# Two products of 512 columns in place of four of 256 in each step of a modulation projection

## The chip, the cores and the metric

The kernel runs on one core of a Trainium2 chip. The metric is the device time in microseconds (us) of one execution. Engines are named as in the profile: PE is the matrix engine (its array is used here as a whole or in four quarters of 32 columns each), PEld is its loading of weights, DVE, ACT and POOL are the vector, scalar and general engines, SP is the engine that issues the loads from memory in its own order.

## What is computed

Two transformer blocks of width 2048 on 256 tokens. The change touches one piece of the second block, the modulation vectors: two rows (the vectors `c` and `c_ctx` after silu) times one matrix of 2048 x 12288 numbers in float32, some 100 MB that are read once.

```python
mod = jax.nn.silu(c) @ mod_w + mod_b
mod_c = jax.nn.silu(c_ctx) @ mod_w + mod_b
sh1, sc1, g1, sh2, sc2, g2 = jnp.split(mod[:, None, :], 6, axis=-1)
csh1, csc1, cg1, csh2, csc2, cg2 = jnp.split(mod_c[None, None, :], 6, axis=-1)
```

## The kernel before

A scheduler orders the instructions of each engine when the program is built; on the chip each engine works through its own list and waits on semaphores.

Most of the work is projections (`proj_t`, `proj_k`, `proj_n`, with `mm3` at L166 to L173): weights come in pieces of 128x1024 (L140), ACT copies each half into a rounded high part (L230), DVE takes the rest as a low part (L231), and PE makes three products for each 128x128 block of weights.

The modulation is filler between these projections. It is a generator, `modulation`, with 12 groups (`q`) of 1024 output columns; a group is 16 steps (`k`), one for each 128 rows of the matrix, so there are 192 steps. A step loads one tile `mw` of 128x1024 (L889; there are two such buffers, so step k's load waits until step k - 2 has been multiplied) and multiplies it by `scw`, 128 rows of 32 columns of which two hold the data and the rest zeros. The weights are thus 32 columns wide, and each of the step's four products of 256 columns stands on its own quarter of the array (`tile_position=(0, 32 * j)`) and writes its own 32 partitions of one accumulator `mps`. A float32 product is two instructions in the trace, two passes over the same columns, so a step is 8 matmul instructions.

After 16 steps ACT copies `mps` to `mrow` (L894), two small products with the identity turn the rows into columns (L897), and DVE adds the bias (L902).

Ten groups are asked for in the first block, by `tick` (two or three steps after each projection), and the last two in the MLP's first half (`MR = 3` steps after each pair of blocks of `w1m`). The first ten run between about 39 and 1000 us, the last two between 2635 and 2776 us.

Of the kernel before, what the change touches and what calls it, by code (L numbers as in the profile page):

```python
# [9 lines left out]
F32 = mybir.dt.float32  # L10
# [7 lines left out]
MUL, ADD, SUB = ALU.mult, ALU.add, ALU.subtract  # L18
# [3 lines left out]
NK = 16  # L22
# [11 lines left out]
PP, S0, S1 = 3, 3, 2  # L34
# [16 lines left out]
def bc(ap, n, axis):  # L51

    l = [list(x) for x in ap.ap]
    l.insert(axis, [0, n])
    return bass.AP(tensor=ap.tensor, offset=ap.offset, ap=l)


class Env:
    def __init__(self, tc, ctx):
        self.tc, self.nc = tc, tc.nc  # L60
        p = lambda name, bufs, **k: ctx.enter_context(tc.tile_pool(name=name, bufs=bufs, **k))
        self.cp = p("consts", 1)
        self.wp = p("weights", 3)
        self.hp = p("acts", 1)
        self.kp = p("work", 2)
        self.dp = p("dram", 1, space=bass.MemoryType.DRAM)
        self.ps = p("psum", 1, space=PSUM)

        self.slot, self.npt, self.held = None, 0, 0
# [773 lines left out]
class Second:  # L843


    def __init__(self, e, a):
        self.e, self.a, nc = e, a, e.nc
        v, g = nc.vector, nc.gpsimd
        c = lambda n, shape, dt=F32: e.cp.tile(shape, dt, name=n, tag=n)
        pv = c("pv2", [128, NPV2])  # L850
        nc.sync.dma_start(pv, a["pv2"])
        self.pv = {n: pv[:, i:j] for n, (i, j) in PV2.items()}
        self.modx, self.modc = c("modx", [128, 96]), c("modc", [128, 32])

        self.scw = c("scw", [128, 16, 32])
        g.memset(self.scw, 0.0)
        for j, n in enumerate(("c", "cc")):
            t = c("silu_" + n, [128, 16])
            nc.scalar.activation(t, self.pv[n], AF.Tanh, scale=0.5)
            v.scalar_tensor_tensor(t, t, 1.0, self.pv[n], op0=ADD, op1=MUL)  # L860
            v.tensor_scalar(self.scw[:, :, j], t, 0.5, None, op0=MUL)

        self.om, self.mu4, self.mu2 = c("om", [128, 28]), c("mu4", [128, 28, 4]), c("mu2", [128, 28, 2])
        mu = self.pv["mu"]
        v.tensor_scalar(self.om, mu, -1.0, 1.0, op0=MUL, op1=ADD)
        v.tensor_tensor(self.mu4, bc(mu, 4, 2), bc(self.pv["m4"], 28, 1), op=MUL)
        v.tensor_tensor(self.mu2, bc(mu, 2, 2), bc(self.pv["m2"], 28, 1), op=MUL)
        d = lambda n, k: e.dp.tile([128, k, T], F32, name=n, tag=n)
        self.zc, self.zx = d("zc", 24), d("zx", 24)
        self.gc, self.gx = d("gcd", 24), d("gxd", 24)  # L870
        self.gz, self.gate, self.x1 = d("gzd", 8), d("gated", 32), d("x1d", 16)
        self.ya, self.yb = d("yad", 8), d("ybd", 8)
        self.at = e.dp.tile([128, 2, 16, 128], F32, name="atd", tag="atd")
        self.twe = {s: c("twe" + s, [97, T]) for s in "cx"}
        self.xa = {s: c("xa" + s, [128, T]) for s in "cx"}
        self.ab = {s: c("ab" + s, [128, 2, 32]) for s in "cx"}
        self.xg = c("xg", [128, 2, T])
        self.state = [d(f"rws{b}", 1) for b in range(4)]


    def modulation(self, mp, groups):


        e, nc = self.e, self.e.nc
        for q in groups:
            ps = e.ps.tile([128, 512], F32, name="mps", tag="s1", bufs=S1)[:, :256]
            for k in range(NK):
                w = mp.tile([128, 1024], F32, name="mw", tag="mw", bufs=2)
                nc.sync.dma_start(w, self.a["mod_w"][k * 128:k * 128 + 128, q * 1024:(q + 1) * 1024])  # L889
                for j in range(4):  # L890
                    nc.tensor.matmul(ps[32 * j:32 * j + 32], self.scw[:, k, :], w[:, j * 256:(j + 1) * 256], start=k == 0, stop=k == NK - 1, tile_position=(0, 32 * j))  # L891
                yield
            rows = mp.tile([128, 256], F32, name="mrow", tag="mrow", bufs=1)
            nc.scalar.copy(rows, ps)  # L894
            p = e.pt()
            for i in range(2):
                nc.tensor.matmul(p[:, 8 * i:8 * i + 8], rows[:, i * 128:(i + 1) * 128], e.ident.rearrange("p (j r) -> p r j", j=4)[:, :2], start=True, stop=True)  # L897
            sl = slice(8 * q, 8 * q + 8)
            by = lambda x: x.rearrange("p (j i) -> p i j", i=2)
            pv = p[:, :16].rearrange("p (i m j) -> p i m j", i=2, m=2)  # L900
            for m, out in enumerate([self.modx] + ([self.modc] if q < 4 else [])):
                nc.vector.tensor_tensor(by(out[:, sl]), pv[:, :, m], by(self.pv["mod_b"][:, sl]), op=ADD)  # L902

# [1034 lines left out]
```

## Time and profile before

| | |
|---|---|
| median of 3 runs | 3372.09 us (3361.31 to 3379.54) |
| the profiled execution's own time | 3366.81 us |
| its span, first to last instruction | 3365.1 us |
| mean granted clock of PE | 0.985 of full speed |
| busy share of PE, DVE, ACT, POOL | 97%, 70%, 47%, 10% |
| moved to and from memory | 640.73 MB, 190 GB/s over the span |

A row of the profile names line, engine, operation, the tile written and those read. Durations are of one instruction; matmuls of one engine overlap in time, so what one costs is read from the start of one piece to the start of the next. In the timeline, neighbouring equal instructions are merged and counted (x8).

### The profile page before, as it was taken

To read this page: it belongs to the slowest core of one execution; us is meant where nothing else is said; L and a number is where in the kernel's file an instruction comes from. 1 tells how busy PE (TensorE), PEld (TensorE's weight loads), DVE (VectorE), ACT (ScalarE), POOL (GpSimd) and SP (SyncE) were. 2 spreads that over 40 slices of the span, in tenths; PEclk is the share of its full clock that TensorE was granted. 3 is DMA by queue.
4 is the path that set the end of the run, shared out by engine and by line. 5 is a ranking of instruction groups with operands and counts; after the bars stand their busy time and mean duration, and the time that the engine had idled before them with its cause. 6 is when DMAs were issued, how large, how long until landed. Compare 5 with 4: busy or idle time off the path is not lost.

```text
span 3365.1 us, 76958 instructions
## 1 busy us (share of the span) xinstructions
PE 3266.7 (97%) x30462; PEld 2997.4 (89%) x30462; DVE 2358.3 (70%) x5132; ACT 1588.5 (47%) x3191; POOL 347.6 (10%) x635
## 2 busy tenths in 40 slices
PE   8999999999999999999999999999999999999998
PEld 6888889988789888889999899899998999899987
DVE  7757766567577687887898588567777555556655
ACT  4444454444344554554555245244455544455553
POOL 1101000001011012111103102102020100001000
PEclk9999999999999998999999999999999999999999
DMA  7777776886765553444545155255576775555554
GB/s 251 226 250 233 255 239 206 267 276 207 254 215 179 172 181 103 126 144 146 162 149 181 63 156 169 78 171 169 163 231 202 252 266 188 188 186 184 183 192 152
DMA packets 224822, 640.73 MB, mean 190 GB/s; under 512 B 24330, under 2 KB 79948, under 8 KB 224332
## 3 DMA queue, kind: packets, MB, share of 16 engines
q1 hardware_dynamic: 224460, 635.81, 58.3%
q8 instruction: 239, 3.92, 0.5%
q14 instruction: 123, 1.01, 0.1%
HBM read 607.78 MB, written 27.93 MB: 189 GB/s over the span
## 4 chain that ended last, share of the span: by engine, by line
PE 85%; DMA 7%; DVE 5%; issue 1%; ACT 1%; POOL 0%; SPq 0%; DVEq 0%; ACTq 0%
PE pp L171 17%; PE pp L173 17%; PE pp L172 17%; PE pp L166 8%; PE pp L167 4%; DMA mw<-in_mod_w 3%; PE mps L891 3%; PE pp L204 2%; PE pp L203 2%; PE pp L205 2%; DVE wl L231 1%; PE sm L1291 1%; PE sm L1342 1%; PE sm L1321 1%; PE sm L1333 1%
## 5 line engine op out<-in xcount | busy, mean ns | idle before, releaser
L231 DVE TENSOR_TENSOR wl<-wr,wh 128x512 fp32r<-128x512 f32 x1752 | 1219.0, 703 | 689.4 <-ACT wh L230 667.0
L230 ACT CAST wh<-wr 128x512 fp32r<-128x512 f32 x1752 | 1074.5, 619 | 1293.3 <-PE pp L172 818.7
L171 PE MATMUL pp<-act,wh 128*128 128x256 f32 x3920 | 1133.1, 290 | 23.7 <-ACT wh L230 18.0
L173 PE MATMUL pp<-act,wl 128*128 128x256 f32 x3920 | 1129.7, 289 | 1.8 <-DVE wl L231 1.8
L172 PE MATMUL pp<-act,wh 128*128 128x256 f32 x3920 | 1129.3, 288 | 1.4 <-DVE act L929 1.4
L171 PEld LDWEIGHTS pp<-act,wh 128*128 128x128 f32 x3920 | 758.6, 194 | 50.1 <-ACT wh L230 24.1
L173 PEld LDWEIGHTS pp<-act,wl 128*128 128x128 f32 x3920 | 758.1, 194 | 20.7 <-issue 8.7
L172 PEld LDWEIGHTS pp<-act,wh 128*128 128x128 f32 x3920 | 759.5, 194 | 13.7 <-issue 7.7
L173 PE MATMUL pp<-mhi,wl 128*128 128x258 f32 x1024 | 291.9, 285 | 0.0
L171 PE MATMUL pp<-mhi,wh 128*128 128x258 f32 x1024 | 290.7, 284 | 0.0
L172 PE MATMUL pp<-mlo,wh 128*128 128x258 f32 x1024 | 288.7, 282 | 0.0
L166 PE MATMUL pp<-act,wh 128*128 128x512 f32 x752 | 266.2, 397 | 0.0
L167 PE MATMUL pp<-act,wl 128*128 128x256 f32 x768 | 212.7, 280 | 0.5 <-DVE wl L231 0.4
L171 PEld LDWEIGHTS pp<-mhi,wh 128*128 128x128 f32 x1024 | 194.8, 190 | 4.5 <-ACT wh L230 3.7
L173 PEld LDWEIGHTS pp<-mhi,wl 128*128 128x128 f32 x1024 | 193.3, 189 | 4.1 <-issue 4.1
L172 PEld LDWEIGHTS pp<-mlo,wh 128*128 128x128 f32 x1024 | 194.7, 190 | 0.5 <-issue 0.4
L166 PEld LDWEIGHTS pp<-act,wh 128*128 128x128 f32 x752 | 141.4, 188 | 31.6
L166 PE MATMUL pp<-u,wh 128*128 128x512 f32 x480 | 168.2, 392 | 0.0
L167 PEld LDWEIGHTS pp<-act,wl 128*128 128x128 f32 x768 | 144.9, 189 | 4.6 <-DVE wl L231 1.4
L167 PE MATMUL pp<-u,wl 128*128 128x256 f32 x512 | 138.1, 280 | 0.0
L891 PE MATMUL mps<-mw,scw 128*32 128x256 f32 x1536 | 122.0, 391 | 14.1 <-DMA mw<-in_mod_w 13.9
L166 PEld LDWEIGHTS pp<-u,wh 128*128 128x128 f32 x480 | 90.1, 188 | 20.3
(529 smaller groups left out, 4602.1 us busy)
## 6 DMA issues: line engine op xcount, KB each, us to landing
wr<-in_in_w SPq DMA_DIRECT2D x252, 512.0 KB, 3.9
wr<-in_w SPq DMA_DIRECT2D x240, 512.0 KB, 4.2
mw<-in_mod_w SPq DMA_DIRECT2D x192, 512.0 KB, 5.9
wr<-in_w1m SPq DMA_DIRECT2D x128, 512.0 KB, 4.3
wr<-in_w2m SPq DMA_DIRECT2D x128, 512.0 KB, 3.2
wr<-in_wo SPq DMA_DIRECT2D x64, 512.0 KB, 4.4
wr<-in_out_w SPq DMA_DIRECT2D x32, 512.0 KB, 3.2
wr<-in_up_a SPq DMA_DIRECT2D x16, 512.0 KB, 3.5
```

Source lines behind the costliest of these rows:

```text
L166: mm(o, hi, h[2][:, k, :], start=k == 0, stop=False)
L167: mm(o[:, :T], lo, h[0][:, k, :], start=False, stop=False)
L171: mm(o, hi, h[0][:, k, :], start=k == 0, stop=False)
L172: mm(o, hi, h[1][:, k, :], start=False, stop=False)
L173: mm(o, lo, h[0][:, k, :], start=False, stop=k == nk - 1)
L203: mm(p[b], x, hi, start=k == 0, stop=False)
L204: mm(p[b], x, wlo, start=False, stop=False)
L205: mm(p[b], xl, hi, start=False, stop=k == nk - 1)
L230: self.nc.scalar.copy(hi, sl)
L231: self.nc.vector.tensor_tensor(lo, sl, hi, op=SUB)
L891: nc.tensor.matmul(ps[32 * j:32 * j + 32], self.scw[:, k, :], w[:, j * 256:(j + 1) * 256], start=k == 0, stop=k == NK - 1, tile_position=( ...
L1291: mm(p4(p)[:, d, t, :], bT[rows[r], t, d, ch[i]], ar[rows[r], t, d, 0, ch[i]], start=True, stop=True)
```

## The change

A step makes two products of 512 columns. Even steps use the array's first two quarters, odd steps the last two, so the accumulator holds the sum over even k in partitions 0 to 63 and over odd k in 64 to 127, and is 512 columns wide. The two sums are added where rows are turned into columns: the identity is replaced by a matrix `sel` with two ones in each column, and there are four small products of 128 columns each instead of two.

```diff
+        self.sel = c("sel", [128, 2, 2])
+        by = e.ident.rearrange("p (a j r) -> p a r j", a=2, j=2)
+        v.tensor_tensor(self.sel, by[:, 0, :2], by[:, 1, :2], op=ADD)
...
-            ps = e.ps.tile([128, 512], F32, name="mps", tag="s1", bufs=S1)[:, :256]
+            ps = e.ps.tile([128, 512], F32, name="mps", tag="s1", bufs=S1)
...
-                for j in range(4):
-                    nc.tensor.matmul(ps[32 * j:32 * j + 32], self.scw[:, k, :], w[:, j * 256:(j + 1) * 256], start=k == 0, stop=k == NK - 1, tile_position=(0, 32 * j))
+                for j in range(2):
+                    i = 64 * (k % 2) + 32 * j
+                    nc.tensor.matmul(ps[i:i + 32], self.scw[:, k, :], w[:, j * 512:(j + 1) * 512], start=k < 2, stop=k >= NK - 2, tile_position=(0, i))
                 yield
-            rows = mp.tile([128, 256], F32, name="mrow", tag="mrow", bufs=1)
+            rows = mp.tile([128, 512], F32, name="mrow", tag="mrow", bufs=1)
             nc.scalar.copy(rows, ps)
             p = e.pt()
-            for i in range(2):
-                nc.tensor.matmul(p[:, 8 * i:8 * i + 8], rows[:, i * 128:(i + 1) * 128], e.ident.rearrange("p (j r) -> p r j", j=4)[:, :2], start=True, stop=True)
+            for i in range(4):
+                nc.tensor.matmul(p[:, 4 * i:4 * i + 4], rows[:, i * 128:(i + 1) * 128], self.sel, start=True, stop=True)
             sl = slice(8 * q, 8 * q + 8)
-            by = lambda x: x.rearrange("p (j i) -> p i j", i=2)
-            pv = p[:, :16].rearrange("p (i m j) -> p i m j", i=2, m=2)
+            by = lambda x: x.rearrange("p (j i) -> p i j", i=4)
+            pv = p[:, :16].rearrange("p (i m j) -> p i m j", i=4, m=2)
```

The lines of the modulation move from L889, L891, L894 and L897 to L893, L896, L899 and L902. The scheduler makes a new order. On PE (a row here is a matmul of the program, which is two instructions in the trace), the place where the first group ends and the second begins stood so before:

```order
L173 MATMUL pp<-act_176,wl 128x256
L171 MATMUL pp<-act_177,wh 128x256
L897 MATMUL sm<-ident,mrow 128x8 x2
L891 MATMUL mps<-mw,scw 32x256 x4
L172 MATMUL pp<-act_177,wh 128x256
L173 MATMUL pp<-act_177,wl 128x256
```

And it stands so now:

```order
L171 MATMUL pp<-act_180,wh 128x256
L172 MATMUL pp<-act_180,wh 128x256
L902 MATMUL sm<-sel,mrow 128x4 x4
L896 MATMUL mps<-mw,scw 32x512 x2
L173 MATMUL pp<-act_180,wl 128x256
L171 MATMUL pp<-act_181,wh 128x256
```

The step stands alone between the products of a projection in both, and the four small products have taken the place of two.

On PE a little later, around the first scores of one attention (`gqe`, `gke`), where a step is cut in two pieces, the order before was this:

```order
L173 MATMUL pp<-act_189,wl 128x256
L891 MATMUL mps<-mw,scw 32x256
L507 MATMUL sm<-gqe,gke 128x128 x8
L891 MATMUL mps<-mw,scw 32x256 x7
L171 MATMUL pp<-act_174,wh 128x256
```

Now it is this:

```order
L173 MATMUL pp<-act_191,wl 128x256
L896 MATMUL mps<-mw,scw 32x512
L507 MATMUL sm<-gqe,gke 128x128 x8
L896 MATMUL mps<-mw,scw 32x512 x3
L171 MATMUL pp<-act_176,wh 128x256
```

The seven products before are the last three of one step and the four of the next; the three now are the last one of an even step and the two of the odd step behind it. The steps keep their places, and so do the pieces.

Counted over the whole of PE's order, the modulation's products stand in 157 separate pieces before and 150 now. Before, 92 pieces are one whole step, 42 are two steps back to back, 17 hold one to three products, and 6 reach over a step's end (a part of one step and some of the next). Now 98 are one whole step (49 even, 49 odd), 43 are two steps back to back (always one even and one odd), 5 hold one product, and 4 reach over a step's end.

## Rows read from the trace of the kernel before

**Rows 1.** Busy time by stretch: engines, granted clock (PEclk), DMA share, GB/s.

```profile
core 0: us, PE busy (x) PEld busy (x) DVE busy (x) ACT busy (x) POOL busy (x), PEclk, DMA share, GB/s
...
50.00:1000.00 950.00, 929.68 (x7490) 809.44 (x7487) 622.83 (x1155) 414.35 (x816) 59.26 (x45) 0.99 0.74 240
1000.00:2600.00 1600.00, 1551.63 (x17308) 1467.40 (x17307) 1251.19 (x3067) 766.86 (x1648) 231.84 (x488) 0.98 0.49 154
2600.00:2780.00 180.00, 180.00 (x1579) 166.06 (x1578) 101.37 (x208) 91.80 (x169) 16.39 (x26) 1.00 0.76 256
```

**Rows 2.** Groups of PE instructions: count, busy us, mean ns, idle before, releaser.

```profile
L171 PE MATMUL pp<-act,wh 128*128 128x256 f32 x3920 | 1133.1, 290 | 23.7 <-ACT wh L230 18.0 <-DVE qT L417 2.6 <-ACT act L305 1.7
...
L891 PE MATMUL mps<-mw,scw 128*32 128x256 f32 x1536 | 122.0, 391 | 14.1 <-DMA mw<-in_mod_w 13.9
L204 PE MATMUL pp<-wl,act 128*128 128x512 f32 x256 | 102.4, 400 | 0.0
```

**Rows 3.** The chain that ended last, from 0 to 1000 us, by line.

```profile
by line: PE pp L173 17.1%; PE pp L171 17.0%; PE pp L172 16.7%; DMA mw<-in_mod_w 9.9%; PE mps L891 7.9%; PE pp L204 4.7%; PE pp L203 4.6%; PE pp L205 4.5%; PE sm L542 1.9%; DMA wr<-in_w 1.7%; issue 1.5%; DVE wl L231 1.3%; DMA cx<-in_ctx 0.9%
```

**Rows 4.** Timeline of PE, a step alone: start us, us, what.

```profile
44.59 0.28 PE L173 MATMUL pp<-act,wl 128*128 128x256 f32 x1
44.71 0.28 PE L171 MATMUL pp<-act,wh 128*128 128x256 f32 x1
44.92 0.64 PE L891 MATMUL mps<-mw,scw 128*32 128x256 f32 x8
45.48 0.39 PE L172 MATMUL pp<-act,wh 128*128 128x256 f32 x1
```

**Rows 5.** Timeline of PE, two steps back to back.

```profile
38.93 1.07 PE L891 MATMUL mps<-mw,scw 128*32 128x256 f32 x16
39.93 0.39 PE L171 MATMUL pp<-act,wh 128*128 128x256 f32 x1
```

**Rows 6.** Timeline of PE, one product alone, and two alone.

```profile
67.80 0.62 PE L891 MATMUL mps<-mw,scw 128*32 128x256 f32 x2
68.35 0.50 PE L204 MATMUL pp<-wl,act 128*128 128x512 f32 x1
...
203.29 0.62 PE L891 MATMUL mps<-mw,scw 128*32 128x256 f32 x4
203.85 0.50 PE L204 MATMUL pp<-wl,act 128*128 128x512 f32 x1
```

**Rows 7.** Timeline of PE: a step's first product, later its other three and the next four.

```profile
131.30 0.62 PE L891 MATMUL mps<-mw,scw 128*32 128x256 f32 x2
...
133.71 1.06 PE L891 MATMUL mps<-mw,scw 128*32 128x256 f32 x14
```

**Rows 8.** The later piece again, only what had started by 133.75 us.

```profile
133.71 0.42 PE L891 MATMUL mps<-mw,scw 128*32 128x256 f32 x4
```

**Rows 9.** Timeline of PE, the two small products at a group's end.

```profile
111.45 0.51 PE L897 MATMUL sm<-ident,mrow 128*128 128x8 f32 x4
111.89 0.64 PE L891 MATMUL mps<-mw,scw 128*32 128x256 f32 x8
```

**Rows 10.** Chain in order of time: the first of eight such links, and the last.

```profile
264.89 0.61 PE mps L891 x8
...
265.52 6.40 DMA mw<-in_mod_w
...
271.96 0.64 PE mps L891 x8
...
971.95 0.61 PE mps L891 x8
```

**Rows 11.** Who waited for the modulation's loads, 0 to 1000 us: total, times, longest.

```profile
PE mps L891 <- DMA mw<-in_mod_w: 13.9, 16, 2.0
```

**Rows 12.** Copies on ACT: durations min/median/max in ns, of two shapes.

```profile
L894 ACT COPY mrow<-mps x12: 355/372/373, 109.2 to 2772.6; 128x256 f32<-128x256 f32 x12
...
L1357 ACT COPY nat<-sm x24: 567/586/594, 1307.6 to 2155.2; 128x512 f32<-128x512 f32 x24
```

## The prediction

> **What bounds the kernel now.** I read the busy time by stretch first, because a filler is worth what it costs in the stretch where it runs. From 50 to 1000 us, where ten of the twelve groups run, PE is busy 929.7 of 950 us, and from 2600 to 2780 us, where the last two run, all of 180 us [rows 1]. The DMA share is 0.74 to 0.76 there, and no other engine comes near. PE bounds both stretches, at a granted clock of 0.99 to 1.00, the upper of its two levels (2.4 GHz).
>
> Second, the groups: the modulation's 1536 matmul instructions keep PE busy for 122.0 us, and the idle time before them is 14.1 us, 13.9 of it for their own load [rows 2]. Third, the chain over the first 1000 us: 7.9% is these products and 9.9% is the load of `mw` [rows 3]. The second figure is no time in which PE stood still: most of such a link lies beside projections that keep PE full, and only its tail is idle.
>
> Then the timeline, for what one step takes from PE. A product of a projection follows the one before after 0.12 us. A step alone starts at 44.92 and the next product at 45.48: 0.56 us, and it starts 0.21 us after its neighbour instead of 0.12 [rows 4]. Two steps back to back take 39.93 - 38.93 = 1.00 us [rows 5], so a further step adds 0.44 us, that is 0.22 for each of its two passes. One product alone takes 0.55 us, two alone 0.56 [rows 6], four 0.56: the four quarters run side by side, and one quarter alone is no faster. So a piece costs its longest quarter: about 0.12 us of entry and exit, and 0.22 us for each pass of 256 columns.
>
> **The change, part by part.**
>
> *The products.* A quarter that is used has 512 columns to stream in a pass instead of 256. No float32 pass of 512 columns stands in the trace. Below, it could cost no more than one of 256 (0.22); above, twice (0.44). The near row is the projection's product: 290 ns with 256 columns, 400 ns with 512 [rows 2], 110 ns for 256 more columns in its single pass, against 0.12 from one such product to the next [rows 4]. Time goes with columns, so I take 0.44, and a step alone becomes 0.56 + 2 x 0.22 = 1.00 us. The two idle quarters earn nothing there, since the product that follows needs the whole array.
>
> A pair of an even and an odd step fills all four quarters. If they run side by side, a pair costs 1.00 us, as two steps do now. Whether quarters overlap across a step's border shows at 131 to 134 us: a step's first product stands alone, and later its other three and the next step's four make one piece of 14 instructions [rows 7]. Within 0.04 us of its start, four were running [rows 8]: three of the one step, and a fourth that can only be the next step's, on the quarter that was free. So pairs overlap.
>
> Now the counts from the program's order. Before: 92 pieces of one step x 0.56 = 51.5; 42 pairs x 1.00 = 42.0; 17 smaller pieces x 0.55 = 9.4; 6 longer ones x 1.00 = 6.0; together 108.9 us. After: all 150 pieces (98 alone, 43 pairs, 9 others) last two passes of 0.44, so 150 x 1.00 = 150.0 us. That is **+41.1 us**. There are 7 pieces fewer, each of which starts 0.09 us late [rows 4]: -0.6.
>
> *The small products.* Four instructions take 111.89 - 111.45 = 0.44 us [rows 9], 0.11 each. Now there are eight, so +0.44 us in each of 12 groups: **+5.3**. Below, nothing, if they were all hidden; above, double.
>
> *The loads.* With two buffers, a load waits for the step before the last. In a pair today the first step frees its buffer 0.61 us after the start and its load is issued at once: the pair starts at 264.89, the load of 6.40 us at 265.52, and the next step at 271.96, just behind it [rows 10]. The chain holds eight links that leave a pair at its half. Now both steps of a pair end together, so that load starts some 0.4 us later and PE waits that much longer: 8 x 0.44 = **+3.5**. Below: PE waits 16 times, 13.9 us [rows 11], and a step alone that lies between a load's issue and its use covers 0.44 us more of it, so it could as well come out at -7 (16 x 0.44). Above: all 43 pairs, +19. I take +3.5, by the links that are seen. SP issues in order, so weights behind a late load are 0.4 us later too. ACT and DVE, which they feed, are busy 44% and 66% of this stretch [rows 1].
>
> *The rest.* The copy to `mrow` doubles to 512 columns: 372 ns against 586 for such a copy elsewhere [rows 12], 12 x 0.21 = 2.6 us on ACT. That engine's idle time hides it; without cover the small products behind it would be 2.6 us late in all. One DVE instruction makes `sel` ahead of the first load: nothing, and 0.2 us if uncovered. The scheduler's new order moves work on other engines too, but the steps keep their places; I take nothing, and 8 us either way for the range.
>
> The sum: 41.1 - 0.6 + 5.3 + 3.5 = **+49 us**. On the profiled execution, 3366.8 + 49 = 3416. Its time lies 5 us under the median shown (3372.1), on which it would be 3421. I say **3418 us**, 1.4% slower.
>
> A rule speaks against these pairs: the Trainium skill, TensorE: Matmul & The Clock Gate, section "Step-by-step: what each phase is for", says that matmuls stay in program order and that only weight loads are pulled ahead. If that held across quarters, an odd step's products would wait behind the even step's second pass. By that rule the sum would be about 19 us more (the second rival). The trace does not agree: four instructions run where order allows three, and two products take 0.56 us where one takes 0.55.
>
> **The rivals.**
>
> *Columns are not what is paid for.* If the quarters shared one stream of the array's input, four at once would slow each other, and two of 512 columns would take as long as four of 256. For it: the same number of values is read in a step. Then a step alone stays at 0.56, a pair at 1.00, and the pieces together take 98 x 0.56 + 43 x 1.00 + 5 x 0.55 + 4 x 1.00 = 105 us, 4 less than before. With the other terms that is -4 - 0.6 + 5.3 + 3.5 = +4, 3373 us, no slower than can be told. It decides if a pass of 512 columns in two quarters takes less than about 0.28 us (98 x 2 x 0.06 = 12 more). Against it: one quarter alone takes 0.55 us, four take 0.56, so nothing is shared that binds.
>
> *Pairs run one after the other.* An odd step's first pass starts only with the even step's second. A pair is three passes long: +0.44 x 43 = +19, so 3437 us. Against it is the piece of 14.
>
> *Waits take it up.* PE's idle time from 50 to 1000 us is 20 us [rows 1], the 13.9 for these loads among it. If longer steps covered all of it, 20 us and the 3.5 would fall away: about +26, 3395 us. For it: at 240 GB/s loads are slow here, and a longer stretch eases them. Against it: a load's wait begins when a step ends, so a longer step pushes it along.
>
> **How the numbers follow.** Forecast 0.80; serial pairs 0.07; covered waits 0.08; columns not paid for 0.05. Half a per cent, 17 us, is about what a measurement of this kernel can tell from no change. The first three are slower than that, the fourth is the same, and I keep 0.01 of it for faster: 0.01, 0.05, 0.94. The forecast's own bounds are 49 - 10.5 - 8 and 49 + 8, with the runs' own spread of some 9 us around them; the range goes from the covered waits to the serial pairs, 3394 to 3440.
>
> **What would show it.** In the changed kernel's timeline, a step alone should take 1.00 us from its start to the next product's, and a piece of two steps (8 instructions) the same; 1.44 for the latter would be the serial rival, 0.56 for the former the first. Eight small products should take 0.88 us. PE's busy time should grow by some 45 us, and its idle time before the modulation's products stay between 7 and 25. If PE's busy time grew so and the time did not, the gain came from waits elsewhere, which the stretch from 1000 to 2600 us (48 us idle [rows 1]) would show.

## The result, and the profile after

The changed kernel takes 3397.69 us (median of 5 runs, 3394.77 to 3405.27) against 3372.09 before: the ratio, taken over all runs of both, is 1.0083, with a 95% interval of 1.0065 to 1.0101 (the two medians alone are 0.76% apart). It is slower, inside the stated range and near its low end. The forecast was 1.4%; 0.8% was measured. The sizes below are read from one profiled execution of each kernel: the span went from 3365.1 to 3397.8 us, +32.7, where the sum had +49. The five runs of the kernel before spread over 18 us, so a few us of such a difference can be spread.

The page's first part of the changed kernel (busy us, share of the span, instructions); before, PE was busy 3266.7 us:

```profile
PE 3303.3 (97%) x29742; PEld 2984.9 (88%) x29742; DVE 2355.4 (69%) x5133; ACT 1594.0 (47%) x3191; POOL 348.9 (10%) x635
```

PE is busy 36.6 us more, where the prediction had some 45, and idle 4 us less. The group of the modulation's products, which answers to the second row of [rows 2], and the wait that answers to [rows 11], now over the whole run:

```profile
L896 PE MATMUL mps<-mw,scw 128*32 128x512 f32 x768 | 158.6, 605 | 8.9 <-DMA mw<-in_mod_w 8.8
```

```profile
PE mps L896 <- DMA mw<-in_mod_w: 8.8, 15, 1.4
```

Half the instructions, 36.6 us more busy time, and 5 us less idle time before them. The timeline of PE in the changed kernel, for a step alone, a pair, and the small products (start us, us, what), answers to [rows 4], [rows 5] and [rows 9]:

```profile
44.91 0.28 PE L172 MATMUL pp<-act,wh 128*128 128x256 f32 x1
45.12 1.05 PE L896 MATMUL mps<-mw,scw 128*32 128x512 f32 x4
46.10 0.38 PE L173 MATMUL pp<-act,wl 128*128 128x256 f32 x1
46.33 0.28 PE L171 MATMUL pp<-act,wh 128*128 128x256 f32 x1
...
38.66 1.06 PE L896 MATMUL mps<-mw,scw 128*32 128x512 f32 x8
39.66 0.38 PE L171 MATMUL pp<-act,wh 128*128 128x256 f32 x1
...
115.05 0.95 PE L902 MATMUL sm<-sel,mrow 128*128 128x4 f32 x8
115.94 1.05 PE L896 MATMUL mps<-mw,scw 128*32 128x512 f32 x4
```

A step alone takes 46.10 - 45.12 = 0.98 us (0.56 before), a pair 1.00 (as before), the eight small products 0.89 (0.44 before for four). Each is within 0.02 us of the prediction.

Where the rest went shows by stretch. The first row of each view runs from the first step to the last of the tenth group, the second to the eleventh group's first step, the third to the last step (columns as in [rows 1]). First the kernel before:

```profile
39.00:995.00 956.00, 935.68 (x7572) 815.41 (x7572) 625.72 (x1172) 414.98 (x808) 59.26 (x45) 0.99 0.74 241
995.00:2635.60 1640.60, 1592.23 (x17627) 1506.26 (x17625) 1279.55 (x3129) 790.37 (x1701) 235.14 (x493) 0.98 0.49 156
2635.60:2772.00 136.40, 136.40 (x1217) 123.05 (x1220) 72.53 (x143) 67.51 (x122) 12.45 (x20) 1.00 0.80 270
```

Then the changed kernel:

```profile
38.60:1012.50 973.90, 966.57 (x6967) 804.99 (x6966) 624.11 (x1172) 418.42 (x807) 61.22 (x45) 1.00 0.72 237
1012.50:2659.30 1646.80, 1591.91 (x17629) 1506.13 (x17627) 1278.35 (x3129) 792.33 (x1701) 234.45 (x493) 0.98 0.49 155
2659.30:2804.50 145.20, 142.37 (x1098) 120.78 (x1096) 72.64 (x144) 67.81 (x123) 12.48 (x20) 1.00 0.77 255
```

The three stretches grew by 17.9, 6.2 and 8.8 us, 32.9 together. In the first, PE's idle time fell from 20.3 to 7.3 us (length less busy time), and the granted clock rose from 0.99 to 1.00. Of these 13.0 us, 8.0 stood before the modulation's own products (14.1 and now 6.1) and 5.0 before other products (6.2 and now 1.3). The second stretch holds no modulation at all, and PE is busy as long as before (1592.2 and 1591.9 us): its 6.2 us are idle time. The scheduler's new order is the likely cause, but it is not shown, since one execution of each cannot tell 6 us from the runs' own spread. In the third, where PE had no idle time, it now waits 2.8 us.

### The profile page after: what moved, and what is told of

It is laid out like the page before. It is cut to its first block, busy times and chain, and to the rows that moved or that the text cites. A ratio compares the mean times of both kernels' runs of the same rounds, so it can differ in the third digit from the quotient of the medians.

```text
span 3397.8 us, 75520 instructions
## 1 busy us (share of the span) xinstructions
PE 3303.3 (97%) x29742; PEld 2984.9 (88%) x29742; DVE 2355.4 (69%) x5133; ACT 1594.0 (47%) x3191; POOL 348.9 (10%) x635
## 4 chain that ended last, share of the span: by engine, by line
PE 88%; DMA 6%; DVE 3%; issue 1%; ACT 0%; POOL 0%; SPq 0%; DVEq 0%; ACTq 0%
PE pp L171 17%; PE pp L173 17%; PE pp L172 17%; PE pp L166 8%; PE mps L896 4%; PE pp L167 4%; DMA mw<-in_mod_w 3%; PE pp L204 2%; PE pp L203 2%; PE pp L205 2%; DVE wl L231 1%; PE sm L1347 1%; PE sm L1338 1%; PE sm L1296 1%; PE sm L1326 1%
## 5 line engine op out<-in xcount | busy, mean ns | idle before, releaser
L896 PE MATMUL mps<-mw,scw 128*32 128x512 f32 x768 | 158.6, 605 | 8.9 <-DMA mw<-in_mod_w 8.8
```

The costliest lines, as they stand in the source:

```text
L896: nc.tensor.matmul(ps[i:i + 32], self.scw[:, k, :], w[:, j * 512:(j + 1) * 512], start=k < 2, stop=k >= NK - 2, tile_position=(0, i))
```

## The experiments

Each was timed against the kernel before on its own chip (medians there 3363 to 3366 us); ratios are to it.

**Without the turn between even and odd steps.**

```diff
-                    i = 64 * (k % 2) + 32 * j
+                    i = 32 * j
...
-            nc.scalar.copy(rows, ps)
+            nc.scalar.copy(rows, ps[:64])
```

(The accumulation starts at step 0 and stops at the last step accordingly, and the small products read 64 partitions and two columns of the identity.)

> The changed kernel, but every step uses the first two quarters of the array (no turn between even and odd), and the small products take the two rows from 64 partitions. In the order that the scheduler makes, 78 pieces are one step and 51 are two steps back to back. Theory (a piece costs its busiest quarter, 0.43 us a pass of 512 columns): a step alone stays at 0.98 us, a pair goes from 1.00 to 1.84 us, the pieces together from 148 to 190 us, so about +42 us over the changed kernel, near 3440. Rival (pairs gain nothing from having quarters of their own): a pair costs the same in both, no difference to the changed kernel, near 3398.

Measured: 3441.72 us, ratio 1.0211 (1.0187 to 1.0235), 44 us above the changed kernel's median, where the theory had 42. The timeline of a pair in this kernel:

```profile
240.31 1.91 PE L896 MATMUL mps<-mw,scw 128*32 128x512 f32 x8
242.15 0.39 PE L171 MATMUL pp<-act,wh 128*128 128x256 f32 x1
```

A pair takes 1.84 us where it took 1.00 with quarters of its own. So the turn is worth 0.84 us, a second step's two passes, and only in pairs: half of the changed kernel's steps (98 of 192) stand alone and gain nothing from it.

**Four products of 256 columns on two quarters.**

```diff
-                for j in range(2):
-                    i = 64 * (k % 2) + 32 * j
+                for j in range(4):
+                    i, n = 64 * (k % 2) + 32 * (j // 2), 256 * (j % 2)
...
+                    nc.tensor.matmul(ps[i:i + 32, n:n + 256], self.scw[:, k, :], w[:, j * 256:(j + 1) * 256], ...
```

> The changed kernel with four products of 256 columns again, two on each of the step's two quarters, one after the other in the program. Theory (columns on the busiest quarter are what is paid for, each quarter works through its own list): a step alone 0.98 to 1.00 us as with two of 512, time as the changed kernel, 3398 within 12 for the new order. Rival one (the length of a product matters): a step is longer by four more passes' fixed cost. Rival two (products keep the program's order over all quarters): the second quarter starts only when the first has its second product running, and a step takes near 1.6 us, some +90 us.

Measured: 3411.57 us, ratio 1.0126 (1.0103 to 1.0149); the profiled execution's span was 3398.8. The median is 14 us above the changed kernel's, a little outside the 12 that were allowed (its four runs go from 3400.55 to 3415.18), but the price of a step is read from the step itself:

```profile
86.09 1.06 PE L896 MATMUL mps<-mw,scw 128*32 128x256 f32 x8
87.08 0.39 PE L173 MATMUL pp<-act,wl 128*128 128x256 f32 x1
```

0.99 us for a step alone, against 0.98 with two products of 512. The length of a product is worth 0.01 us a step; what costs is that two quarters carry all columns. And the second quarter did not wait for the first: that would have been near 1.6 us, by the estimate above. The rule of program order for matmuls (the Trainium skill, TensorE: Matmul & The Clock Gate, section "Step-by-step: what each phase is for") does not hold across quarters here.

**Three buffers for the modulation's weights, in the kernel before and in the changed one.** The room comes from `HM`, the number of buffers of the tile `hmod`, in which the context's input is scaled.

```diff
-EK, HM = 8, 4
+EK, HM = 8, 2
...
-                w = mp.tile([128, 1024], F32, name="mw", tag="mw", bufs=2)
+                w = mp.tile([128, 1024], F32, name="mw", tag="mw", bufs=3)
```

> The kernel before with three buffers for the modulation's weights instead of two (the room comes from two buffers less for one tile of the context's input). The scheduler now bunches the steps: 98 pieces instead of 157, by the same row prices 105 us instead of 110. Waits for these loads, 16 us before the products and 6 us behind them, should nearly vanish. Theory of waits: 5 + some 18 us less, near 3350. Rival (that idle time only moves to other loads or to the weights): 5 us less, near 3367.

> The changed kernel with the same three buffers: 90 pieces, 128 us by the row prices (three steps in a piece are two passes' turns on one half and one on the other, 1.84 us), against 105 in the kernel before with three buffers. With the waits gone from both, the difference of the two should be the price of the products alone: 23 us for the pieces and 5 for the small products, +28. Theory that the longer steps covered waits in the changed kernel: here nothing is left to cover, so +28 in full. Rival (the missing time was the luck of the order elsewhere): anything from +15 to +40, and the stretch without modulation between the tenth and the eleventh group shows it.

Measured: 3333.46 us for the kernel before with three buffers, ratio 0.990 (0.9877 to 0.9922), and 3361.97 us for the changed one, ratio 0.9989 (0.9977 to 1.0001). The modulation's products in the first and the second of the two:

```profile
L891 PE MATMUL mps<-mw,scw 128*32 128x256 f32 x1536 | 111.9, 385 | 0.8 <-DMA mw<-in_mod_w 0.7
```

```profile
L896 PE MATMUL mps<-mw,scw 128*32 128x512 f32 x768 | 134.3, 602 | 0.0
```

With the waits gone from both, the difference of the medians is 28.5 us, as the row prices gave (23 + 5). The profiled spans differ by 38.2 (3363.1 and 3324.9), but these are the slowest of ten runs and the fastest of four. In the two stretches with modulation they differ by 19.7 and 4.4 us (938.9 and 137.3 against 919.2 and 132.9), with 2.9 us less idle time in the first: some 27 for the products. Another 11.9 lies in the stretch without modulation, 1654.8 us long in the one and 1642.9 in the other. So the prices hold where there is nothing to cover. What made the 11.9, the order there or the spread of the runs, is open.

The first of the two beats the kernel before by 1%. Its gain of some 32 us was more than the 23 expected. In its first stretch (36.5 to 955.7 us, 919.2 us long) PE is idle 7 us instead of 20, the granted clock is 1.00 instead of 0.99, and there are 49 pieces fewer. Each of these would have cost 0.19 us at its borders, which the row prices leave out (see the products' price in the next part), some 9 us in all.

**Control: the buffers that made the room.** The kernel before with `HM = 2` and nothing else.

> Control for the runs with three buffers: the kernel before with two buffers instead of four for the modulated context's tile, nothing else. If that tile's buffers are off the path, no change, 3366 within 8, and the waits for the modulation's loads stay near 16 us. If they bind, part of what three buffers gave or cost is theirs.

Measured: 3364.88 us, ratio 0.9994 (0.9979 to 1.001): no change. PE waits 17.1 us for the loads there, and is idle 22.8 us in all in the first stretch (959.7 us, 936.9 busy), as the kernel before was (13.9 and 20.3). So the smaller tile gave none of the gain, and the idle time is no accident of one order.

**Every product of the kernel before made twice.** The second copy goes to columns 256 to 511 of the accumulator and is not read.

```diff
+                for n in (0, 256):
...
-                    nc.tensor.matmul(ps[32 * j:32 * j + 32], self.scw[:, k, :], ...
+                        nc.tensor.matmul(ps[32 * j:32 * j + 32, n:n + 256], self.scw[:, k, :], ...
```

> The kernel before, with every product of the modulation made twice (the second into columns of the accumulator that nobody reads). All four quarters stay in use; a step alone becomes 1.00 us, a pair 1.86. By the program's order and the row prices the pieces cost 82 us more than before. Theory (longer steps on PE cover the loads, which begin when a step ends): the waits for these loads fall from 16 us to some 5 and the slow-clock stretches behind them go, so +65, near 3431. Rival (the waits fell in the changed kernel because its pairs free both buffers at once, or by luck of the order): the waits stay near 16 us and the time rises by the whole 82, near 3448.

Measured: 3441.61 us, ratio 1.0226 (1.0203 to 1.0249), +76 us, between the two (+65 and +82). The group there, and its wait for the load:

```profile
L892 PE MATMUL mps<-mw,scw 128*32 128x256 f32 x3072 | 203.4, 384 | 10.9 <-DMA mw<-in_mod_w 10.4
```

PE waits 10.4 us for the loads, not 5 and not 16; no slow clock shows in its first stretch after 41 us. So longer steps do cover part of the waits, but not as much as went in the changed kernel.

**Four buffers in the kernel before**, with `EK, HM = 5, 2` (`EK` is the number of context tiles that are prepared early).

> The kernel before with four buffers for the modulation's weights (room from two buffers less of the context's tile and three early context tiles less). 96 pieces, 102 us by the row prices, as with three buffers. Theory that three buffers already took every wait for these loads: as the kernel before with three, 3333 within 10. Rival (a deeper queue of loads brings more): some 5 to 10 us less.

Measured: 3350.86 us, ratio 0.9957 (0.994 to 0.9974): 17 us slower than with three, outside the 10 allowed. The stretch without modulation, with three buffers and then with four:

```profile
955.70:2598.60 1642.90, 1598.33 (x17672) 1509.84 (x17665) 1282.10 (x3137) 793.50 (x1703) 237.21 (x494) 0.98 0.49 156
...
957.40:2626.00 1668.60, 1608.43 (x17670) 1518.55 (x17662) 1287.35 (x3137) 793.86 (x1703) 238.62 (x494) 0.97 0.49 154
```

The first and third stretches are as with three buffers (920.8 and 133.0 us against 919.2 and 132.9), so the fourth buffer bought nothing there. The second is 25.7 us longer: PE is busy 10 us more, at a lower granted clock, and idle 15.6 us more. `EK` was changed along with the buffers and no run has it alone, so whether `EK` or the new order did this is open. By the medians the difference is 17 us, since the profiled execution with three buffers was the fastest of its four, and with four the slowest of its eight.

## Why the prediction was right, and where it was off

The range held, but the forecast of 3418 us was 20 us too high. The mechanism of the largest term, the products, was right; the term of the waits was not, and the clock had no term. Part of what these had wrong was made up elsewhere, which is luck.

*The products' price: right.* A piece costs its busiest quarter. In the first stretch the pieces, at these prices, went from 93 to 126 us (135 and 128 pieces), in the third from 17 to 22, in all +38 against +41 predicted. No float32 pass of 512 columns had been in the trace; it takes the upper of the two bounds. (Only float32 products are two instructions each; in the order rows of the part on the change, those of the projections are one.) Pairs overlap across a step's border, as the piece of 14 in [rows 7, 8] had shown, and the experiment without the turn shows what they would cost otherwise. The sum left out one border: not only does a piece start 0.21 us behind its neighbour, the second product after it too comes 0.23 us after the first (46.10 to 46.33 above), where 0.12 is usual. A piece thus costs 0.09 + 0.10 us beyond what the prices count. With 7 pieces fewer that is -1.3 instead of -0.6.

*The small products: right.* 0.81 to 0.89 us for eight instead of 0.36 to 0.44 for four, some 0.45 more a group, +5.3 for the 12.

*The loads: the step that failed.* By the profiled spans the sum was 16 us too high. The step "8 x 0.44 = +3.5" gave waits that grow behind pairs, with -7 to +19 as bounds. The waits before the modulation's products fell by 5.2 us over the whole run instead (14.1 to 8.9 us: -8.0 in the first stretch, +2.8 in the third), inside the bounds but with the other sign. Another 5.0 us of idle time before other products, which had no term, went in the first stretch. The idle time just before each piece, by what piece of the modulation stood before it (a longer piece is more than one step):

| kernel | behind a step alone | behind a longer piece |
|---|---|---|
| before | 4.8 us in 6 | 9.2 us in 11 |
| before, `HM = 2` | 7.1 us in 7 | 7.5 us in 12 |
| changed | none | 8.8 us in 15 |
| four of 256 on two quarters | none | 10.4 us in 18 |
| without the turn | none | 5.2 us in 7 |
| every product twice | 2.6 us in 8 | 8.3 us in 20 |

Behind a step alone the wait goes in all three kernels with two quarters per step. The lone step between a load's issue and its use is 0.42 us longer there and covers that much, the case that the prediction had only as a bound; but that is 6 x 0.42 = 2.5 of the 4.8 us at most, and with every product made twice the lone step is as long and 2.6 us stay. What differs as well is the load itself. Matched issue by issue, loads that are used behind a step alone in the first stretch took 6.0 us (median) from issue to landing before, 6.2 with `HM = 2`, 5.9 with every product twice, and 5.3 to 5.4 in the three kernels with two quarters. Why they land sooner there is open.

Behind longer pieces the waits are there as said, and in the third stretch plainly so: all seven, 2.8 us, stand behind a pair. One of them in the changed kernel's timeline, with the idle time before the step and its releaser:

```profile
2680.15 0.28 PE L172 MATMUL pp<-mlo,wh 128*128 128x258 f32 x1
2681.21 1.05 PE L896 MATMUL mps<-mw,scw 128*32 128x512 f32 x4 [0.78 <-DMA mw<-in_mod_w]
```

In the first stretch the waits behind longer pieces did not grow (9.2 to 6.1 us). Over all loads the median from issue to landing fell from 5.8 to 5.4 us, and doubling the products gave 5.6. (The page's medians for these loads, 5.9 and 5.0, rest on 22 and 24 of the 192.)

*The clock, which the prediction left out.* The kernel before lost some 5 us to slow stretches of the clock in the first stretch, and the changed kernel none (last part). With it, the first stretch closes: pieces +33.3, small products +4.0, borders of 7 pieces fewer -1.3, idle time -13.0, clock -4.7, together +18.3, where 17.9 was measured.

*Elsewhere.* The prediction took nothing and 8 us either way. It was +6.2 in the profiled execution, inside the bound, and it hid part of the error on the waits and the clock. The bound was too narrow for this program in general: in the nine profiled executions the stretch without modulation took between 1641 and 1669 us, though no run tells how much of that is order and how much spread.

*The rivals.* That columns are not what is paid for fell with the first step alone, and serial pairs fell with the first pair. "Waits take it up" came closest, at 3395 us for 3397.7 measured, closer than the forecast. But it is not what happened as it was put: 13 of the 20 us of idle time went in the first stretch and 2.8 us came in the third, longer steps are shown to cover only part of that, and part of the rival's sum was made up by the clock.

## What to carry to other kernels

A float32 product split over quarters of PE's array costs what its busiest quarter streams, so columns should be spread over all four in every step that may stand alone; leaving half the array to the next step pays only where the program's order puts that step right behind. The order that the scheduler made, counted piece by piece, told beforehand that two pieces in three would be a step alone. Here, where the filler's own loads made PE wait with the engine else full, one more buffer gained 1%, while all three arrangements of its products on two quarters lost with the two buffers. The buffer took away waits and also let the scheduler bunch the steps into fewer pieces, each of which costs PE at its borders. A longer step hid part of such a wait (10.4 us with every product twice, 13.9 before), so the price of the added work was not fully paid.

## What the runs showed of the hardware

PE's clock went to its lower level (1.2 GHz, half of the upper) at some of PE's waits. The granted clock in the kernel before, around the wait of 1.4 us that ends at 181.4 us and the one of 1.7 us that ends at 903.6 (columns as in [rows 1]):

```profile
170.00:181.00 11.00, 9.03 (x80) 7.92 (x78) 6.03 (x14) 3.27 (x6) 0.00 (x0) 0.99 0.89 260
181.00:188.00 7.00, 6.59 (x35) 5.79 (x36) 2.44 (x5) 1.23 (x2) 0.00 (x0) 0.53 0.88 297
...
895.00:905.00 10.00, 8.27 (x76) 7.07 (x73) 4.22 (x7) 4.09 (x8) 0.00 (x0) 0.97 0.82 266
905.00:908.00 3.00, 3.00 (x19) 1.97 (x18) 0.00 (x0) 0.00 (x0) 0.00 (x0) 0.53 0.63 188
```

Ten microseconds at 0.53 cost 10 x 0.47 = 4.7 us, more than the two waits themselves (3.1 us). In the page's 40 slices such a stretch does not show; it has to be looked for behind the waits. In the nine traces there are nine such stretches between 42 us and the tenth group's end. Each begins in or shortly after a wait of PE of 1.3 to 2.6 us, for `mw` or for a projection's weights. But the changed kernel had a wait of 1.4 us too, which ended at 868 us, and the kernel before its longest, 2.0 us, which ended at 348.2, and both kept the upper level: the wait's length alone does not decide.

And the quarters of the array take their products each in its own order: products that stand behind others in the program start at once on a quarter that is free, across steps and across the two passes of a float32 product, as the pair (1.00 us) and the step of four on two quarters (0.99 us) show.
